# A two-layer streaming encoder in FP32 on one core: twelve of the mixer's sixteen output rows taken by seven products instead of eight

## The chip, the cores and the metric

The kernel runs on one core of one Trainium2 chip. The metric is the device time of one launch in microseconds (us). The engines are called TensorE (PE in the profile, its weight loads PEld), VectorE (DVE), ScalarE (ACT), GpSimd (POOL) and SyncE (SP, which only starts transfers here).

## The reference

Two layers work on 640 tokens (512 new frames of one stream and 16 new frames of each of eight running streams), 1024 wide. Each layer is a half-step SwiGLU block, the mixer, and a second half-step SwiGLU block; a last norm follows. The change lies in the mixer's second half:

```
z = h @ w_in                       # conv B | C | V | q | k | v | gates (2 x 1024 columns)
y_c = B * causal_depthwise_conv3(C * V)          # 512 wide
y_a = chunk-band attention(q, k, v)              # 512 wide
m = sigmoid(g_c) * (y_c @ w_conv_out) + sigmoid(g_a) * (y_a @ w_attn_out)
x += m @ w_o
```

## The kernel before

Everything is feature-major: a tile is 128 features by 640 tokens, cut into two halves of 320 tokens (`t1`, `t2`). Operands are split into a high part (a rounding copy on ACT, names ending in `hi`) and a low part (the rest, `source - hi`, on DVE, names ending in `lo`), and each product is three matmuls: high by high, high by low, low by high. One matmul is 128x128 by 128x320.

**Products by seven.** The FFN's and the mixer's input products use a 2x2 block scheme with seven block products instead of eight. A *unit* makes two output rows. It has seven blocks of 12 matmuls, 84 in all, in this order; I number them here:

| block | operand | written to (PSUM) | weights |
|---|---|---|---|
| P1 | `X11` | `pa` | w0 |
| P2 | `X21` | `pb` | w0 |
| P3 | `XN6` | `pa`, added on | w1 |
| P4 | `XT5` | `pc` | w1 |
| P5 | `XT7` | `pa`, added on | w2 |
| P6 | `X22` | `pc`, added on | w2 |
| P7 | `XT4` | `pa`, added on | w3 |

Since `pa` is added on, P3 waits until ACT has copied P1's sum out (`c1`), P5 until ACT has copied the next one (`u2`), and P7 until DVE has used P5's sum (`add(g[:, t2], pa, c5)`).

**Weights.** A unit's weights arrive as two tiles `raw` of 128x1024 (n and n + 1, three buffers in all). `source` makes sums of them on DVE, `prep` splits them into `whi` and `wlo` (three buffers each) for the slabs w0 to w3, and `slab`, `quiet` and `flush` say where in DVE's queue that is written. Of w1 the first half (the sum `s6`) serves P3, the second P4; of w2 the first half serves P5. In a mixer unit DVE makes three sums for w1 and w2's first half, and one more for w2's second half.

**The stage.** `outputs` runs with PE, DVE and ACT in the order of the program text. It makes seven gate units (`gate_pair(2)` to `gate_pair(14)`, each with two sigmoids on ACT) and 16 output rows: 8 of `y_c @ w_conv_out` (`co`), 8 of `y_a @ w_attn_out` (`ao`), each row by `out`: 24 matmuls on `py`, then a product with the gate on DVE, and for `ao` a sum into `mm`. After gate 2 come rows 0 to 3, and after each later gate unit two rows. `give` splits the eight results `mm` into the operands `m_0` to `m_7` of the last product, `po` = w_o, 48 matmuls for each of 8 rows. The tiles of `m_0` to `m_7` are those of the normalised input `h`, which the gate units' blocks P1, P2, P4 and P6 read.

Of the kernel before, what the change touches and what calls it, by code (L numbers as in the profile page):

```python
# [59 lines left out]
MARGIN = 2, 4  # L60
LEAN = {"a0": (1, 6), "b0": (1, 5), "a1": (0, 5), "b1": (1, 5)}
# [52 lines left out]
def mixer_order():  # L114

    mix = lambda *rows: ("mix", rows)
    out = [("v", None)] + [mix(("q", p), ("k", p)) for p in range(AW // P)]
    for c in range(0, CT, 2):  # L120
        out += [mix(("C", c + i), ("V", c + i)) for i in range(2)] + [mix(("B", c), ("B", c + 1))]
    gates = [mix(("g", m), ("g", m + 1)) for m in range(0, 2 * KT, 2)]
    out += gates[:2] + [("co", m) for m in range(4)]
    for i, g in enumerate(gates[2:]):
        name, m = ("co", 4 + 2 * i) if i < 2 else ("ao", 2 * i - 4)
        out += [g, (name, m), (name, m + 1)]
    return out + [("o", m) for m in range(KT)]
# [8 lines left out]
def stages():  # L136

    out, done = [], []

    def end(kind):  # L140
        done.append((kind, out[:]))
        out.clear()

    def plain(n):
        out.extend([8] * (n // 8) + [n % 8] * (n % 8 > 0))

    def ffn(name):
        held = 0
        for what, a in ffn_order(name):
            if what == "gu":  # L150
                plain(held)
                held = 0
                out.append("gu")
            elif what == "std":
                held += 2 * KT
            elif what == "cut":
                plain(held)
                held = 0
            elif what == "rows":
                plain(held)  # L160
                held = 0
                out.append("gu")
            elif what == "ends":
                held += KT * len(a)
            else:
                held += sum(len(js) for _, js in a)
        plain(held)

    for l in range(L):
        ffn(f"a{l}")  # L170
        end("ffn")
        held = 0
        for what, _ in mixer_order():
            if what == "mix":
# [12 lines left out]
def two(ps):  # L187
    return ps[:, :, :HT]
# [7 lines left out]
def trunk(ctx: ExitStack, tc: tile.TileContext, xin, wst, small, pbias, samplebias, kcache, vcache, gfin,  # L196
# [54 lines left out]
    for kind, units in stages():  # L251
# [3 lines left out]
        at += n  # L255
    raws, ready = [], []
    sums, pool, spool = {}, [None], [None]
    lent, lean, at = {}, set(), 0
    for name, (_, units) in zip([f"{k}{l}" for l in range(L) for k in "amb"], stages()):
        ns = []  # L260
        for z in units:
            if z == "gu":
                ns.append(at)
            at += 2 if z in ("gu", "mix") else 1
        if name in LEAN:
            lean.update(ns[slice(*LEAN[name])])

    def lend(n):

        z = lent[n] = pool[0].tile([P, 2, HT], F32, tag="cap", name=f"lent{n}", bufs=6).rearrange(  # L270
            "p a b -> p (a b)")[:, h1]
        POOL.dma_start(z, wst[n][:, h1])
# [20 lines left out]
    def source(i):  # L293
# [3 lines left out]
        if i not in sources:  # L297
# [4 lines left out]
            elif arg == 0:  # L302
                if n in lean and n not in lent:
                    lend(n)
                sources[i] = [(ra, whole)]
            else:
                rb = load(n + 1)
                if arg == 1 and kind == "gu":
# [5 lines left out]
                    sources[i] = [(st, whole)]  # L314
                elif arg == 1:
# [1001 lines left out]
    def mixer(l, after):  # L1317
        with tc.tile_pool(name=f"yp{l}", bufs=1, reuse_waits="tile") as yp, \
# [84 lines left out]
            with tc.tile_pool(name=f"gp{l}", bufs=1, reuse_waits="tile") as gp, \  # L1403
                 tc.manual_schedule(engines=ORDERED):
                hold[0] = True
                mo = outputs(l, gp, ops.X, st, cs, ycs, yas, sigmoid, gates)
        ex = after()
        with tc.manual_schedule(engines=ORDERED):
            hold[0] = True
            for m in range(KT):  # L1410
                po = acc(f"po{l}_{m}")
                product(po, mo)
# [56 lines left out]
    def outputs(l, gp, X, st, cs, ycs, yas, sigmoid, gates):  # L1469
# [4 lines left out]
        mm = ycs + [spare[i // 2][:, i % 2] for i in range(CT)]  # L1474
# [4 lines left out]
        def gate_pair(m, then=None):  # L1479
# [5 lines left out]
            ACT.copy(c1, pa)  # L1485
            prep(used[0] + 1)
            flush()
            block(pb, s0, 1, X21, every, True, True)
# [6 lines left out]
            ACT.copy(c5, pc)  # L1495
            s2 = slab(True)[0]
# [5 lines left out]
            if then:  # L1502
                then()
# [4 lines left out]
            sigmoid(u, m)  # L1508
# [5 lines left out]
            sigmoid(g, m + 1, -1.0)  # L1514
# [7 lines left out]
        def out(m, y, then=None):  # L1522

            py = acc(f"py{l}_{m}")
# [9 lines left out]
            flush()  # L1534

        yc, ya, mo = [], [], []

        def take(y, name, srcs):
            for c, src in enumerate(srcs):
                y.append(parts(gp, f"y{c}", f"{name}{l}_{c}", src))  # L1540
# [5 lines left out]
        gate_pair(2, lambda: take(yc, "yc", ycs))  # L1546
        for m in range(4):
            out(m, yc)
        for m in range(4, 2 * KT, 2):
            last = m == 2 * KT - 2  # L1550
            gate_pair(m, (lambda: take(ya, "ya", [yas[:, c, :] for c in range(CT)])) if m == KT else
                      (lambda: give(range(1))) if last else None)
            y = yc if m < KT else ya
            out(m, y, (lambda: give(range(1, 4))) if last else None)
            out(m + 1, y, (lambda: give(range(4, 6))) if last else None)
        give(range(6, KT))
# [520 lines left out]
def _stream(i):  # L2077
# [9 lines left out]
    for l in range(L):  # L2087
# [36 lines left out]
        for what, m in mixer_order():  # L2124
            if what == "v":
                out.append(v.reshape(KT // 2, 2, P, AW).transpose(0, 2, 1, 3).reshape(-1, P, CH))
            elif what == "mix":
# [3 lines left out]
                out.append(chunks([rows[name][a][o::2] for name, a in m for o in range(2)]))  # L2131
            else:
# [73 lines left out]
```

## Time and profile before

| what | us |
|---|---|
| median of 3 runs (2488.70 to 2489.98) | 2489.67 |
| the profiled execution's own time | 2488.93 |
| its span in the trace | 2487.1 |
| from P2's start in gate 2 to the first matmul of `po`, layer 0 (637.35 to 778.09) | 140.74 |
| the same, layer 1 (1869.15 to 2009.89) | 140.74 |

The span's own trace is used for all durations. A row of a timeline gives the start, the duration, the engine, the line, the operation and its tiles; a bracket at its end gives the idle time in front and what ended it. Successive instructions of one engine overlap a little, so what one costs its queue is the distance from its start to the next start, not its duration.

### The profile page before, as it was taken

The numbers are of one execution on the slowest core, as the hardware profiler recorded it, in microseconds if no ns is written. First come the engines' busy times: TensorE is split into PE (matmuls) and PEld (weight loads), VectorE is DVE, ScalarE is ACT, GpSimd is POOL, SyncE is SP. The second block draws the span as 40 slices with busy tenths as digits, with TensorE's granted clock in tenths as the row PEclk, the third lists the DMA queues.
The fourth block names the chain that finished last, engine by engine and source line by source line (L and its number), as shares of the span: only waits on it lengthen the run. The fifth ranks groups of instructions, "written<-read, shape, count | busy, mean of one in ns | idle before, by whom it ended". The sixth has DMA issues, their size and how long they took to land.

```text
span 2487.1 us, 43918 instructions
## 1 busy us (share of the span) xinstructions
PE 2473.8 (99%) x17312; PEld 2421.2 (97%) x17312; DVE 2140.1 (86%) x3533; ACT 1355.4 (54%) x2152; POOL 298.4 (12%) x451
## 2 busy tenths in 40 slices
PE   9999999999999999999999999999999999999999
PEld 8999999889999999999999999998999999999998
DVE  7999998888776899998799999988886769999997
ACT  6555556665444655555665555556644455555555
POOL 0111112211000001111001011121110000111111
PEclk9999999999999999999999999999999999999999
DMA  4443545335223333444334443453442232444444
GB/s 155 126 118 101 124 118 121 113 108 174 77 82 114 93 102 105 113 117 117 111 93 109 110 118 101 116 128 106 133 157 86 77 111 87 109 116 105 113 117 117
DMA packets 109934, 279.75 MB, mean 112 GB/s; under 512 B 12480, under 2 KB 52032, under 8 KB 109728
## 3 DMA queue, kind: packets, MB, share of 16 engines
q1 hardware_dynamic: 69552, 220.10, 28.0%
q0 software_dynamic: 39744, 56.60, 12.3%
q8 instruction: 135, 2.21, 0.4%
q14 instruction: 71, 0.58, 0.1%
q10 hardware_dynamic: 432, 0.25, 0.0%
HBM read 231.09 MB, written 7.94 MB: 96 GB/s over the span
## 4 chain that ended last, share of the span: by engine, by line
PE 94%; DVE 3%; ACT 2%; issue 1%; DMA 1%; SPq 0%; DVEq 0%; ACTq 0%; POOLq 0%
PE pab L442 12%; PE paa L442 11%; PE pcb L442 6%; PE daa L1127 6%; PE pca L442 5%; PE dab L1127 5%; PE po L418 5%; PE py L418 5%; PE qa L442 4%; PE pbb L442 3%; PE dca L1127 3%; PE pba L442 3%; PE dcb L1127 2%; PE ma_cv L442 2%; PE ma_qk L442 2%; PE pv L1612 2%
## 5 line engine op out<-in xcount | busy, mean ns | idle before, releaser
L352 DVE TENSOR_TENSOR wlo<-raw,whi 128x1024 fp32r<-128x1024 f32 (+1 forms) x569 | 579.9, 1021 | 155.9 <-ACT whi L347 152.8
L347 ACT CAST whi<-raw 128x1024 fp32r<-128x1024 f32 (+1 forms) x569 | 504.7, 890 | 380.1 <-PE pbb L442 47.2
L347 ACT CAST whi<-s 128x1024 fp32r<-128x1024 f32 (+1 forms) x158 | 150.3, 951 | 296.1 <-issue 111.2
L442 PE MATMUL pab<-xhib,whi 128*128 128x320 f32 x704 | 217.7, 309 | 0.0
L442 PE MATMUL pab<-xhib,wlo 128*128 128x320 f32 x704 | 217.3, 309 | 0.0
L442 PE MATMUL pab<-xlob,whi 128*128 128x320 f32 x704 | 217.3, 309 | 0.0
L442 PE MATMUL paa<-xhia,whi 128*128 128x320 f32 x640 | 197.8, 309 | 0.2 <-DVE ga L287 0.2
L442 PE MATMUL paa<-xhia,wlo 128*128 128x320 f32 x640 | 197.6, 309 | 0.0
L442 PE MATMUL paa<-xloa,whi 128*128 128x320 f32 x640 | 197.5, 309 | 0.0
L352 DVE TENSOR_TENSOR wlo<-s,whi 128x1024 fp32r<-128x1024 f32 (+1 forms) x158 | 173.5, 1098 | 4.6 <-ACT whi L347 4.6
L1149 POOL DMA_DIRECT2D x<-c_a x80 | 70.2, 1030 | 574.1 <-ACT ahia L1031 205.4
L442 PEld LDWEIGHTS pab<-xhib,whi 128*128 128x128 f32 x704 | 132.2, 188 | 0.9 <-issue 0.9
L1149 POOL DMA_DIRECT2D x<-c_b x72 | 63.2, 1013 | 582.0 <-ACT ahib L1031 205.6
L442 PEld LDWEIGHTS pab<-xlob,whi 128*128 128x128 f32 x704 | 132.2, 188 | 0.0
L442 PEld LDWEIGHTS pab<-xhib,wlo 128*128 128x128 f32 x704 | 132.2, 188 | 0.0
L442 PEld LDWEIGHTS paa<-xhia,whi 128*128 128x128 f32 x640 | 120.1, 188 | 1.1 <-DVE ga L287 0.5
L442 PEld LDWEIGHTS paa<-xloa,whi 128*128 128x128 f32 x640 | 120.2, 188 | 0.3 <-DVE xloa L686 0.3
L442 PEld LDWEIGHTS paa<-xhia,wlo 128*128 128x128 f32 x640 | 120.1, 188 | 0.2
L442 PE MATMUL pcb<-xhib,wlo 128*128 128x320 f32 x352 | 108.9, 309 | 0.0
L442 PE MATMUL pcb<-xlob,whi 128*128 128x320 f32 x352 | 108.6, 309 | 0.0
L442 PE MATMUL pcb<-xhib,whi 128*128 128x320 f32 x352 | 108.6, 309 | 0.0
L287 DVE TENSOR_TENSOR raw<-s,raw 128x512 f32<-128x512 f32 x158 | 107.9, 683 | 0.0
(764 smaller groups left out, 8077.7 us busy)
## 6 DMA issues: line engine op xcount, KB each, us to landing
raw<-in_wst SPq DMA_DIRECT2D x375, 512.0 KB, 3.6
x<-c_a POOLq DMA_DIRECT2D x80, 160.0 KB, 4.7
x<-c_b POOLq DMA_DIRECT2D x72, 160.0 KB, 3.6
lent<-in_wst POOLq DMA_DIRECT2D x36, 256.0 KB, 3.9
kc<-in_kcache SPq DMA_DIRECT2D x32, 256.0 KB, 4.9
vc<-in_vcache SPq DMA_DIRECT2D x16, 512.0 KB, 4.9
x<-u_a POOLq DMA_DIRECT2D x40, 160.0 KB, 3.9
x<-u_b POOLq DMA_DIRECT2D x36, 160.0 KB, 3.9
```

What stands on the lines that cost most here:

```text
L287: DVE.tensor_tensor(out=out, in0=a, in1=b, op=op)
L347: ACT.copy(hi[:, d], src[:, c])
L352: DVE.tensor_tensor(out=lo, in0=src, in1=hi.bitcast(F32), op=ALU.subtract)
L418: PE.matmul(ps[:, a, :HT], w, x[a] if isinstance(x, tuple) else x[:, a * HT : (a + 1) * HT], start=first and j == 0 and not seeded, stop=l ...
L442: PE.matmul(ps, a, b, start=start and kp == 0 and j == 0, stop=stop and kp == NP - 1 and j == 2, skip_group_check=True)
L1127: PE.matmul(ps[u], w, y, start=start and i == 0 and j == 0, stop=i == 1 and j == 2, skip_group_check=True)
L1149: POOL.dma_start(x[ms[2 * u + r]][:, cols], z[:, u], accum_op=ALU.add)
L1612: PE.matmul(pv[t], xx[:, t * P : (t + 1) * P], w[:, kk * AW : (kk + 1) * AW], start=c == 0 and kk == 0 and j == 0, stop=c == KT // 2 - 1 a ...
```

## The change

Rows 4 to 7 of `co` and all rows of `ao` are made by seven, four rows at a time: `rows` is a unit of 84 matmuls where four calls of `out` have 96. The order becomes gate 2, rows 0 to 3, gate 4, gate 6, `co` 4 to 7, gate 8, gate 10, `ao` 0 to 3, gate 12, gate 14, `ao` 4 to 7. The operands for it are made from `y_c` and `y_a` by `mixed` (four sums of 128x320, then splits of 128x960 and 128x320 into high and low parts), twice for each. For the nine units of weights from gate 4 on, one sum that DVE made comes from two transfers on POOL's queue, the second adding onto the first (`lend_one`), issued a unit ahead. The gates' sigmoids are put off into the next unit (`lates`, `due`), the gated rows go through a staging tile, the results of `co` 4 to 7 are copied on ACT (`moved`), and the first two rows of `po` are interleaved by halves of their sums.

```diff
+FREE = AW // P + 3 * CT // 2 + 2
...
+    out += gates[:2] + [("co", m) for m in range(4)] + gates[2:4] + [("rows", ("co", (4, 5, 6, 7)))]
+    for i in range(2):
+        out += gates[4 + 2 * i : 6 + 2 * i] + [("rows", ("ao", tuple(range(4 * i, 4 * i + 4))))]
...
+        lean.update(ns[slice(*LEAN.get(name, (FREE, None)))])
...
+    def lend_one(n):
+        z = lent[n] = apart[0].tile([P, CH // 2], F32, tag="one", name=f"one{n}", bufs=2)
         POOL.dma_start(z, wst[n][:, h1])
         POOL.dma_start(z, wst[n + 1][:, h1], accum_op=ALU.add)
...
+                elif arg == 1 and n in lean:
+                    if after_mix[n] in lean:
+                        lend_one(after_mix[n])
+                    flush()
+                    st = sums[n] = spool[0].tile([P, CH // 2], F32, tag="s6", name=f"s6_{n}", bufs=1)
+                    add(rb[:, h1], rb[:, h1], rb[:, h2])
+                    add(st, rb[:, h1], ra[:, h1])
+                    sources[i] = [(st, h1), (rb, h1)]
...
             block(pa, s0, 0, X11, every, True, True)
             ACT.copy(c1, pa)
+            due()
             prep(used[0] + 1)
             flush()
+            at[0]()
...
-            sigmoid(u, m)
+            lates.append(lambda: sigmoid(u, m))
...
+            first = [acc(f"po{l}_{m}") for m in range(2)]
+            ws = [[tiles.take() for _ in mo] for _ in first]
+            for ks in (range(KT // 2), range(KT // 2, KT)):
+                for p, w in zip(first, ws):
+                    for k in ks:
+                        multiply(p, w[k], mo[k], k == 0, k == KT - 1)
...
+        def mixed(i, y, z):
+            z = z.rearrange("p c (a b) -> p (c a) b", a=2)
+            e1, e2, o1, o2 = (z[:, i] for i in range(4))
+            add(e1, e1, e2, ALU.subtract)
+            add(e2, o2, e2, ALU.subtract)
+            for out, a in ((o2, e1), (o1, o2)):
+                DVE.scalar_tensor_tensor(out=out, in0=a, scalar=-1.0, in1=out, op0=ALU.mult, op1=ALU.subtract)
+            yield
...
+        def rows(name, ms, y, then=None):
...
+            B, A = (acc(f"r{i}{n}") for i in "ba")
+            a, b = ([z[:, u, :HT] for u in range(2)] for z in (A, B))
+            c = [att(f"rc{n}_{u}")[:, :HT] for u in range(2)]
+            s1, s2, s5 = stage
...
+            w = quiet()
+            mul(a, w, 0, X11, True)
+            ACT.copy(s1, two(A))
+            due()
+            prep(used[0] + 1)
+            flush()
+            mul(b, w, 1, X21, True)
+            add(s1, two(B), s1)
+            w = slab(True)[0]
+            flush()
+            mul(a, w, 0, XN6, False)
+            ACT.copy(s2, two(A))
+            gated(0, [s1[:, u] for u in range(2)], t1)
+            mul(c, w, 1, XT5, True)
+            for u in range(2):
+                ACT.copy(s5[:, u], c[u])
+            w = slab(True)[0]
+            mul(a, w, 0, XT7, False)
+            add(s5, two(A), s5)
+            flush()
+            ahead()
+            gated(1, [s5[:, u] for u in range(2)], t2, -1.0)
+            mul(c, w, 1, X22, False)
+            for u in range(2):
+                add(s2[:, u], c[u], s2[:, u])
+            w = slab(True)[0]
+            gated(0, [s2[:, u] for u in range(2)], t2)
+            if then:
+                then()
+            if name == "co":
+                moved(0)
+            mul(a, w, 0, XT4, False)
+            flush()
+            gated(1, a, t1, -1.0)
+            if name == "co":
+                lates.append(lambda: moved(1))
...
+        rows("co", (4, 5, 6, 7), yc)
+        z = [mixed(i, ya, yas[:, 2 * i : 2 * i + 2]) for i in range(2)]
+        pair = lambda c: (take_even(c, yas_[c]), take(ya, "ya", [c + 1], yas_))
+        go = [going(u) for u in z]
+        gate_pair(8, [lambda: pair(0), lambda: pair(2), go[0]])
+        gate_pair(10, [also(go[0], go[1]), also(go[0], go[1], go[0]), also(go[1], go[0], go[1], go[1])])
+        rows("ao", (0, 1, 2, 3), ya)
+        gate_pair(12, [lambda: total(0, 2), none, lambda: total(2, 4)])
+        gate_pair(14, [lambda: give(range(2)), none, lambda: give(range(2, 4))])
+        rows("ao", (4, 5, 6, 7), ya, lambda: total(4, 6))
+        total(6, 8)
+        give(range(4, KT))
```

The three functions given to `gate_pair` run behind P1, behind P4 and behind P5. So the queues of DVE and ACT read otherwise. The rows below are those of layer 0.

DVE before, from the sum of gate 8's P5 (`qa0_8`) on (`wlo190` is the weights of the two rows behind gate 8, `wlo191` w0 of gate 10, the last row the first of gate 10's sums; `ya0_0lo` to `ya0_3lo` are the low parts of the attention's result):

```order
L287 TENSOR_TENSOR g0_8_1_7936<-qa0_8_7932,c50_4829 128x320
L1499 TENSOR_TENSOR g0_8_1_7936<-g0_8_1_7936,rrm0_4818 128x320
L352 TENSOR_TENSOR wlo190_8001<-raw104_7998,whi190_8000 128x1024
L235 TENSOR_TENSOR ya0_0lo_8021<-ya0_4760,ya0_0hi_8020 128x640
L235 TENSOR_TENSOR ya0_1lo_8025<-ya0_4760,ya0_1hi_8024 128x640
L235 TENSOR_TENSOR ya0_2lo_8029<-ya0_4760,ya0_2hi_8028 128x640
L235 TENSOR_TENSOR ya0_3lo_8033<-ya0_4760,ya0_3hi_8032 128x640
L287 TENSOR_TENSOR g0_8_7935<-qc0_8_7934,capsm0_4817 128x320
L1507 TENSOR_TENSOR g0_8_7935<-g0_8_7935,rrm0_4818 128x640
L1513 TENSOR_TENSOR g0_8_1_7936<-qa0_8_7932,rrm0_4818 128x320
L352 TENSOR_TENSOR wlo191_8050<-raw105_8018,whi191_8049 128x1024
L287 TENSOR_TENSOR raw105_8018<-raw105_8018,raw106_8070 128x512
```

DVE now, from the second sum of the weights behind gate 8's P5 on (`wlo193` is w1 of gate 10, its first row the half that P3 waits for; `wlo194` is w2; the two pairs of `x2` rows are `mixed`):

```order
L295 TENSOR_TENSOR s6_104_8099<-raw105_8094,raw104_8074 128x512
L295 TENSOR_TENSOR ya0_4760<-ya0_4760 128x320 x2
L1597 SCALAR_TENSOR_TENSOR ya0_4760<-ya0_4760 128x320 x2
L295 TENSOR_TENSOR g0_8_7991<-qc0_8_7990,capsm0_4817 128x320
L1543 TENSOR_TENSOR g0_8_7991<-g0_8_7991,rrm0_4818 128x640
L1549 TENSOR_TENSOR g0_8_1_7992<-qa0_8_7988,rrm0_4818 128x320
L368 TENSOR_TENSOR wlo193_8120<-s6_104_8099,whi193_8119 128x512
L368 TENSOR_TENSOR wlo193_8120<-raw105_8094,whi193_8119 128x512
L295 TENSOR_TENSOR raw104_8074<-s6_104_8099,raw104_8074 128x512
L368 TENSOR_TENSOR wlo194_8161<-one104_7942,whi194_8160 128x512
L368 TENSOR_TENSOR wlo194_8161<-raw104_8074,whi194_8160 128x512
L295 TENSOR_TENSOR ya0_4760<-ya0_4760 128x320 x2
```

Before, two rows of `out` (48 matmuls) stood between gate 8 and gate 10; now gate 10 follows at once, and the sums for `mixed` stand ahead of its w1.

ACT before, around the start of gate 8 (line 1485 copies `c1`, line 1493 `u2`):

```order
L347 CAST whi187_7875<-raw103_7869 128x512
L1485 COPY capsm0_4817<-qa0_8_7932 128x320
L347 CAST whi188_7951<-raw102_7833 128x1024
L347 CAST whi189_7968<-raw103_7869 128x512
L1493 COPY capsm0_4817<-qa0_8_7932 128x320
```

ACT now at the same place, the start of gate 8 behind `co` 4 to 7 (line 1654 is `moved`, 1519 copies `c1`, 1529 `u2`):

```order
L1654 COPY yc0_0_4819<-g0_4_7588 128x640
L1654 COPY yc0_0_4819<-g0_4_1_7589 128x640
L1519 COPY capsm0_4817<-qa0_8_7988 128x320
L1654 COPY yc0_1_4820<-g0_6_7721 128x640
L1654 COPY yc0_1_4820<-g0_6_1_7722 128x640
L363 CAST whi190_8009<-one102_7810 128x512
L363 CAST whi190_8009<-raw102_7921 128x512
L234 CAST ya0_0hi_8015<-ya0_4760 128x320
L234 CAST ya0_1hi_8019<-ya0_4760 128x640
L363 CAST whi191_8036<-raw103_7940 128x512
L1529 COPY capsm0_4817<-qa0_8_7988 128x320
```

Between the two copies that gate 8's P3 and P5 wait for there stood two casts of weights; now two moves and five casts stand there.

ACT before, around the start of gate 14:

```order
L1485 COPY capsm0_4817<-qa0_14_8509 128x320
L347 CAST whi203_8528<-raw111_8408 128x1024
L347 CAST whi204_8545<-raw112_8444 128x512
L1493 COPY capsm0_4817<-qa0_14_8509 128x320
L1495 COPY c50_4829<-qc0_14_8511 128x320
```

ACT now at the same place (`m0_0hi` and `m0_1hi` are written to tiles of `h` that P4 of this very unit still reads):

```order
L1519 COPY capsm0_4817<-qa0_14_8556 128x320
L1350 ACTIVATE g0_12_8426<-g0_12_8426,sm_73 128x640
L1350 ACTIVATE g0_12_1_8427<-g0_12_1_8427,sm_73 128x640
L363 CAST whi206_8577<-one110_8379 128x512
L363 CAST whi206_8577<-raw110_8493 128x512
L234 CAST m0_0hi_8583<-mm0_0_7299 128x640
L234 CAST m0_1hi_8587<-mm0_0_7299 128x640
L363 CAST whi207_8604<-raw111_8513 128x512
L1529 COPY capsm0_4817<-qa0_14_8556 128x320
```

The first two results' casts moved ahead of the copy of `u2`, and the sigmoids of gate 12 into gate 14.

More of the change, by code (lines that the diff above doesn't have):

```diff
@@ L173, in stages @@
         for what, _ in mixer_order():
[L174 removed]
+            if what in ("mix", "rows"):
                 plain(held)
@@ new lines, in total, with also, going @@
+        def total(m0, m1):
+            for m in range(m0, m1):
+                add(mm[m], mm[m], gates[KT + m])
+        none = lambda: None
+        def also(*fs):
+            return lambda: [f() for f in fs]
+        def going(z):
+            return lambda: next(z)
+        gate_pair(2, [none, none, lambda: take(yc, "yc", range(CT), ycs)])
+        z = [mixed(i, yc, ycp[i]) for i in range(2)]
+        out(0, yc, None, going(z[0]))
+        out(1, yc, None, also(going(z[0]), going(z[1])))
```

123 lines of the change are left out of this document (91 added, 32 removed).

## The prediction

> **What bounds the kernel now.** The page first, then the busy times of the two stretches that change (P2 of gate 2 to the first matmul of `po`, layers 0 and 1), then the chain that ended last inside one of them.
>
> ```profile
> span 2487.1 us, 43918 instructions
> PE 2473.8 (99%) x17312; PEld 2421.2 (97%) x17312; DVE 2140.1 (86%) x3533; ACT 1355.4 (54%) x2152; POOL 298.4 (12%) x451
> ```
>
> ```profile
> core 0: us, PE busy (x) PEld busy (x) DVE busy (x) ACT busy (x) POOL busy (x), PEclk, DMA share, GB/s
> 637.35:778.09 140.74, 140.67 (x962) 140.44 (x960) 100.94 (x144) 65.53 (x96) 0.00 (x0) 1.00 0.27 87
> 1869.15:2009.89 140.74, 140.67 (x962) 140.44 (x960) 100.69 (x143) 65.36 (x96) 0.00 (x0) 1.00 0.26 87
> ```
>
> ```profile
> 637.35 1.76 PE qb L442 x12
> 639.11 1.76 PE qa L442 x12
> ...
> 647.90 14.08 PE py L418 x96
> ...
> 732.30 7.04 PE py L418 x48
> ```
>
> TensorE is the bound, here without a gap: 140.67 of 140.74 us, at full granted clock (1.00). DVE is busy for 100.94 us, 72%. A matmul costs 7.04 / 48 = 0.1467 us, a block of 12 1.76, a unit of 84 12.32.
>
> **What is removed.** Three groups per layer go from 96 to 84 matmuls: 36 x 0.1467 = 5.28 us, 10.56 in both layers. That is all PE can win; against it stand the waits that PE gets.
>
> **What DVE and ACT get.** Their prices are distances from start to start. DVE in a dense piece, then ACT:
>
> ```profile
> 728.89 0.49 DVE L287 TENSOR_TENSOR g<-qa,c 128x320 f32<-128x320 f32 x1 [1.01 <-PE qa L442]
> 729.42 0.49 DVE L1499 TENSOR_TENSOR g<-g,rrm 128x320 f32<-128x320 f32 x1
> 729.83 1.22 DVE L352 TENSOR_TENSOR wlo<-raw,whi 128x1024 fp32r<-128x1024 f32 x1
> 730.96 0.48 DVE L287 TENSOR_TENSOR g<-qc,capsm 128x320 f32<-128x320 f32 x1
> 731.48 0.82 DVE L1507 TENSOR_TENSOR g<-g,rrm 128x640 f32<-128x640 f32 x1
> ...
> 734.00 0.69 DVE L287 TENSOR_TENSOR raw<-raw,raw 128x512 f32<-128x512 f32 x1
> 734.72 0.69 DVE L287 TENSOR_TENSOR s<-raw,raw 128x512 f32<-128x512 f32 x1
> 735.33 0.68 DVE L287 TENSOR_TENSOR raw<-raw 128x512 f32<-128x512 f32 x1
> 735.93 0.82 DVE L1532 TENSOR_TENSOR g<-py,g 128x640 f32<-128x640 f32 x1
> 736.78 0.82 DVE L287 TENSOR_TENSOR yc<-yc,g 128x640 f32<-128x640 f32 x1
> 737.53 0.69 DVE L352 TENSOR_TENSOR wlo<-s,whi 128x512 fp32r<-128x512 f32 x1
> ```
>
> ```profile
> 708.05 1.05 ACT L347 CAST whi<-raw 128x1024 fp32r<-128x1024 f32 x1
> 708.99 0.73 ACT L234 CAST ya_0hi<-ya 128x640 fp32r<-128x640 f32 x1
> 709.62 0.73 ACT L234 CAST ya_1hi<-ya 128x640 fp32r<-128x640 f32 x1
> ...
> 719.00 0.62 ACT L347 CAST whi<-s 128x512 fp32r<-128x512 f32 x1 [1.51 <-DVE s L287]
> 719.53 0.62 ACT L347 CAST whi<-raw 128x512 fp32r<-128x512 f32 x1
> 721.79 0.43 ACT L1485 COPY capsm<-qa 128x320 f32<-128x320 f32 x1 [1.64 <-PE qa L442]
> ```
>
> On DVE 320 columns cost 0.41 us (729.42 to 729.83), or 0.53 where the next instruction needs the result (728.89 to 729.42); 512 cost 0.61 or 0.72, 640 0.74 (736.78 to 737.53) or 0.85, 1024 1.13. On ACT 512 cost 0.53, 640 0.63, 1024 0.94, 320 (not shown alone) about 0.33 as duration less the same 0.1. `mixed` and the gated rows bring two forms that this stretch lacks, which the trace has elsewhere:
>
> ```profile
> 1254.55 1.16 DVE L686 TENSOR_TENSOR xloa<-xoa,xhia 128x960 fp32r<-128x960 f32 x1 [0.32 <-ACT xhia L617]
> 1255.63 0.69 DVE L352 TENSOR_TENSOR wlo<-lent,whi 128x512 fp32r<-128x512 f32 x1
> 1256.23 0.69 DVE L352 TENSOR_TENSOR wlo<-raw,whi 128x512 fp32r<-128x512 f32 x1
> L1154 DVE SCALAR_TENSOR_TENSOR x<-dab,x 128x320 f32<-128x320 f32 x12 | 5.3, 484 | 0.7 <-PE dab L1127 0.5
> ```
>
> 960 columns cost 1.08; the scalar form of 320 columns lasts 0.484, as the plain one. By the order DVE does 52 more instructions of 320 columns, 30 more of 512, 4 of 960, and 8 fewer each of 640 and 1024 per layer: 52 x 0.45 + 30 x 0.61 + 4 x 1.08 - 8 x 0.76 - 8 x 1.13 = +31 us. So DVE has some 101 + 31 = 132 us of work in 140.74 - 5.28 = 135.5. The lent sums are already taken off in this (one of 512 less in each of six gate units, 6 x 0.61 = 3.7 us). The share alone stalls nothing; where the work stands does.
>
> How a late result of DVE or ACT reaches PE is seen once in the FFN:
>
> ```profile
> 1256.33 0.31 PE L442 MATMUL pca<-xloa,whi 128*128 128x320 f32 x1
> 1256.97 0.42 PE L442 MATMUL pca<-xhia,wlo 128*128 128x320 f32 x1 [0.33 <-DVE wlo L352]
> 1257.22 0.31 PE L442 MATMUL pca<-xhia,whi 128*128 128x320 f32 x1
> ```
>
> The low half ended at 1256.92, the held matmul started 0.05 later, and the one behind it came 0.25 after that instead of 0.15. So a matmul whose input ends at time t starts at t + 0.05, and 0.11 more is lost. The low half is first used by a block's third matmul, so it may end 0.13 after the block's due start; an ACT copy must end 0.16 ahead of it. From a block's end to DVE's first use of its sum go 0.27 us, counted from the next block's start:
>
> ```profile
> 728.62 0.31 PE L442 MATMUL qc<-hhim,whi 128*128 128x320 f32 x1
> ```
>
> (728.62 to 728.89, where DVE stood waiting.)
>
> **Five places, per layer.** *1. DVE from gate 8's P5 to P3 of `ao` 0 to 3.* PE passes 24 + 84 + 24 = 132 matmuls, 19.36 us; less 0.27, plus 0.13, DVE has 19.2. In that it must do 36 instructions: 19 of 320 columns (10 held by their forerunner: 5.3 + 3.7), 11 of 512 (two held, the last in full: 7.0), two each of 640, 960 and 1024 (1.5 + 2.2 + 2.3), and it waits 0.1 for a cast: 22.1. PE waits 2.9, part before gate 10's P3, part before that of `ao`. What hid such work before was the 48 matmuls of `py` between two gates, now gone.
>
> *2. ACT into gate 8.* From P5 of `co` 4 to 7, DVE reaches the last gated product that `moved` needs after 0.74 + 1.13 + 0.72 + 0.61 + 6 x 0.41 + 2 x 0.61 + 0.49 = 7.4; behind it ACT does two moves, two casts of 512, one of 320, one of 640, one of 512 and the copy of `u2`: 3 x 0.63 + 3 x 0.53 + 0.33 + 0.43 = 4.24. Gate 8's P5 is due 72 matmuls after the first P5, 10.56 - 0.27 - 0.16 = 10.1. Wait: 11.6 - 10.1 = 1.5.
>
> *3. P3 of gate 14 and of `ao` 4 to 7.* From P5's sum to the low half of the next w1 DVE does 7.26 us (the gate's own 5.78 and two of 640: totals, or the low parts of `m_2`, `m_3`); PE needs it after 48 matmuls, 7.04 - 0.27 + 0.13 = 6.9. Twice 0.36 = 0.7. A unit without extras has 5.78 and a group of rows 6.4: no wait.
>
> *4. P5 of gate 14.* `m_0`'s tile is free after 15 matmuls from P3's start (2.2 + 0.2 us); then two casts of 640, one of 512 and the copy: 2.2 us, end at 4.6; P5 is due at 3.52 - 0.16. Wait 1.3.
>
> *5. The second row of `po`.* It takes the PSUM of `ao` 4 to 7 and waits for the last gated product. Behind P5 DVE does 0.74 + 1.13 + 2 x 0.41 + 4 x 0.41 + 2 x 0.8 + 1.13 + 0.41 + 0.49 = 8.0; due after 48 matmuls, 7.04 - 0.27 - 0.16 = 6.6. Wait 1.3. The interleaving itself then hides `m_4` to `m_7`: their low parts come 0.74 apart, PE needs one per 6 matmuls, 0.88.
>
> Sum 2.9 + 1.5 + 0.7 + 1.3 + 1.3 = 7.7, both layers 15.4, against 10.56: +4.8 us. The profiled execution was 2488.93 us (2487.1 span and 1.8 around it) and becomes 2493.8; the median is 0.74 above it: **2494.5 us**, slower by 0.2%, which is also what a measurement of this kernel can tell from no change.
>
> What I cost at nothing. POOL's lent sums: their like in the FFN has this row.
>
> ```profile
> lent<-in_wst POOLq DMA_DIRECT2D x36, 256.0 KB, 3.9
> ```
>
> Two in turn take 7.8 us and the issue, within the unit of 12.32 by which they are ahead; POOL had 0.00 us to do in the stretch and nothing else is queued there. If they came later than that, w2's cast would stand in ACT's queue, and P5 with it, by the excess. Everything before gate 8: by the same prices DVE has 14.5 us of work beside the 14.08 of the four `py` rows, with gate 2's slack ahead of them, and in gates 4 and 6 one sum less than before. The put-off sigmoids: their results are used a unit later at the earliest. SP's queue has the same loads as before.
>
> **The skill.** The Trainium skill, "VectorE: DVE Perf Modes", section "The DRAIN you can't avoid", says that the next DVE operation does not start until the pipe is empty, semaphore or not. The rows agree only where the next needs the result (0.53 for 0.49); elsewhere the start comes 0.08 earlier, and its own note on instructions that are not held leaves room for that. By the rule place 1 would take the full durations, 23.5 us instead of 22.1.
>
> **The rivals.** *Faster.* Only the two waits behind ACT's queue (places 2 and 4) stay, because DVE runs further ahead than my start at P5 allows: 2 x 2.8 = 5.6 against 10.56, 2484.7 or below. It decides if DVE's 36 instructions take 19 us instead of 22, 0.53 each for 0.61. For it: three buffers of split weights. Against: the distances repeat to 0.01, and P5's sum holds the queue in each unit. 0.10. *Half of it.* Some waits overlap, 8 to 13 us in all: 2487 to 2492. 0.20. *Full durations.* Place 1 takes 9.3 + 7.5 + 1.6 + 2.3 + 2.4 + 0.4 = 23.5 and the others 0.5 more each: 3.3 per layer, 2501. Against: the rows above. 0.03. *Late tiles.* With three `raw` buffers the second tile of a unit is loaded only when DVE has done the w2 before it, 2.7 us into the unit; its sum starts at 7.4.
>
> ```profile
> raw<-in_wst SPq DMA_DIRECT2D x23, 512.0 KB, 3.4
> vc<-in_vcache SPq DMA_DIRECT2D x16, 512.0 KB, 4.9
> ```
>
> At 3.4 us to landing 1.3 are left; beside the lent transfers (256 KB twice) it may be 4.9 or more, then 0.3 in each of six units, 3.6 in all: 2498. 0.12. *The forecast*, 2492 to 2497: 0.55.
>
> **The numbers.** Slower by over 0.2% (above 2494.65) takes half of the forecast's case and some, and both slow rivals: 0.46. Within 0.2%: the other half and the half case, 0.43. Faster 0.11. The range runs from 2487.5 to 2499.
>
> **What would show it.** In the changed trace the stretch should last 135.5 + 7.7 = 143 us, DVE over 90% busy from gate 8 to gate 12, with PE waiting for `wlo` (DVE) at P3 of gate 10 and of `ao`, for ACT's `u2` copy at P5 of gates 8 and 14, and for DVE at `po`'s second row. If PE shows no gap there, the time is 2479; if it waits for a transfer, the late tiles are right.

## The result, and the profile after

The changed kernel takes 2492.38 us (median of 20 runs, 2491.87 to 2493.58) against 2489.11 for the kernel before (20 runs): a ratio of 1.0014, 95% interval 1.0008 to 1.0020. It is slower by 3.3 us, less than the 0.2% set as the bound; the forecast was 2494.5, the range 2487.5 to 2499.0.

The page of the profiled execution, then the two stretches from P2 of gate 2 to the first matmul of `po` and the part of layer 0 from gate 8 to gate 12 (columns as in the view of before: length, then busy time of PE, PEld, DVE, ACT and POOL):

```profile
span 2491.8 us, 44037 instructions
PE 2468.9 (99%) x17240; PEld 2411.7 (97%) x17240; DVE 2193.9 (88%) x3671; ACT 1392.0 (56%) x2236; POOL 323.6 (13%) x487
```

```profile
638.40:779.61 141.21, 137.71 (x926) 135.34 (x925) 125.26 (x207) 81.95 (x135) 10.05 (x14) 1.00 0.38 109
1872.11:2013.63 141.52, 138.03 (x926) 135.62 (x925) 126.41 (x209) 82.46 (x135) 10.06 (x14) 1.00 0.38 109
699.80:740.81 41.01, 38.56 (x255) 36.98 (x253) 38.78 (x69) 25.70 (x44) 4.30 (x6) 1.00 0.44 118
```

The 72 matmuls are gone (17312 to 17240), and yet the stretch lasts longer than the 140.74 us of before. DVE went from 100.94 to 125.26 us, and between gate 8 and gate 12 it is busy for 38.78 of 41.01 us, 95%.

Where TensorE lost time is read best from its weight loads. Matmuls follow each other every 0.147 us but last 0.31, so part of a delay disappears in their overlap; a load lasts 0.19. The last matmul ahead of one wait, and the two behind it:

```profile
730.40 0.31 PE L1640 MATMUL rbao<-ya_3hi,wlo 128*128 128x320 f32 x1
731.14 0.41 PE L1640 MATMUL raao<-xhi,whi 128*128 128x320 f32 x1 [0.43 <-ACT capsm L1658]
731.39 0.30 PE L1640 MATMUL raao<-xlo,whi 128*128 128x320 f32 x1
```

The held matmul starts 0.59 us late, and the next one comes 0.25 behind it instead of 0.147: 0.70 us are lost. The matmul's own bracket says 0.43, that of its load 0.70. These are all the brackets of the timeline of PEld in layer 0 from gate 8 to the second row of `po`:

```profile
703.60 0.19 PEld L458 LDWEIGHTS qa<-thi,whi 128*128 128x128 f32 x1 [0.39 <-ACT capsm L1519]
708.15 0.19 PEld L458 LDWEIGHTS qa<-thi,whi 128*128 128x128 f32 x1 [1.02 <-ACT capsm L1529]
718.04 0.19 PEld L458 LDWEIGHTS qa<-thi,wlo 128*128 128x128 f32 x1 [0.80 <-DVE wlo L368]
721.63 0.19 PEld L458 LDWEIGHTS qa<-thi,whi 128*128 128x128 f32 x1 [0.37 <-ACT capsm L1529]
731.14 0.19 PEld L1640 LDWEIGHTS raao<-xhi,whi 128*128 128x128 f32 x1 [0.70 <-ACT capsm L1658]
732.20 0.19 PEld L1640 LDWEIGHTS raao<-xhi,wlo 128*128 128x128 f32 x1 [0.76 <-DVE wlo L368]
757.13 0.19 PEld L458 LDWEIGHTS qa<-thi,wlo 128*128 128x128 f32 x1 [0.30 <-DVE wlo L368]
761.59 0.19 PEld L458 LDWEIGHTS qa<-thi,whi 128*128 128x128 f32 x1 [1.23 <-ACT capsm L1529]
770.99 0.19 PEld L1640 LDWEIGHTS raao<-xhi,wlo 128*128 128x128 f32 x1 [0.30 <-DVE wlo L368]
784.24 0.30 PEld L434 LDWEIGHTS po<-m_0hi,whi 128*128 128x128 f32 x2 [1.22 <-issue]
```

L1519 and L1529 are ACT's copies `c1` and `u2` of a gate, L1658 the first copy of a group of rows, L368 the low part of weights on DVE; the last, "issue", waits for the last gated product (the matmul's own row names DVE `g`). They add up to 7.1 us, and the view of waits gives the same 7.1 for layer 1. The first nine, 5.87 us, lie in the stretch and account for its length: 140.74 less the 5.28 removed, less 0.3 lost before (shown below), plus 5.87 is 141.0; measured are 141.2 and 141.5. All ten belong to the five chains of the forecast, but three stand at waits that it did not name: P3 of gate 8, P5 of gate 10, and ACT's copy ahead of P3 of `ao`. They lie on the way to the end of a chain, for which the forecast gives the whole delay, so they are added up here:

| place | forecast | measured |
|---|---|---|
| 1: P3 and P5 of gate 10, P3 of `ao` 0 to 3 | 2.9 | 0.80 + 0.37 + 0.70 + 0.76 = 2.6 |
| 2: P3 and P5 of gate 8 | 1.5 | 0.39 + 1.02 = 1.4 |
| 3: P3 of gate 14 and of `ao` 4 to 7 | 0.7 | 0.30 + 0.30 = 0.6 |
| 4: P5 of gate 14 | 1.3 | 1.2 |
| 5: second row of `po` | 1.3 | 1.2 |

What the forecast left out is a wait that the kernel before has and the changed one hasn't. In the same view of the kernel before, PE's loads wait 0.5 us per layer at `po`, 0.3 of it ahead of its first matmul:

```profile
PEld po L418 <- issue: 0.3, 1, 0.3
PEld po L418 <- DVE m_6lo L235: 0.2, 1, 0.2
```

The 0.3 shows in the forecast's own row, where PEld is busy for 140.44 of 140.74 us; it read "without a gap" from the matmuls.

So the account is 2 x (7.1 - 0.5) - 10.6 = +2.6 us; the medians give +3.3, and what makes the 0.7 between them stays open. The two profiled spans differ by 4.7, as the profiled execution of the changed kernel is 1.2 us above its median. It reached P2 of gate 2 at 638.40 instead of 637.35, 1.05 us late in code that the change leaves alone, and lost 0.4 more just ahead of layer 1's P2 of gate 2, where DVE waits for a tile of weights:

```profile
1868.72 0.69 DVE L295 TENSOR_TENSOR raw<-raw,raw 128x512 f32<-128x512 f32 x1 [1.36 <-DMA raw<-in_wst]
1870.35 0.19 PEld L458 LDWEIGHTS qa<-hhim,whi 128*128 128x128 f32 x1 [0.42 <-ACT ya L1999]
```

### The profile page after: what moved, and what is told of

Same layout as the page of the kernel before. It is cut to its first block, busy times and chain, and to the rows that moved or that the text cites. A ratio compares the mean times of both kernels' runs of the same rounds, so it can differ in the third digit from the quotient of the medians.

```text
span 2491.8 us, 44037 instructions
## 1 busy us (share of the span) xinstructions
PE 2468.9 (99%) x17240; PEld 2411.7 (97%) x17240; DVE 2193.9 (88%) x3671; ACT 1392.0 (56%) x2236; POOL 323.6 (13%) x487
## 3 DMA queue, kind: packets, MB, share of 16 engines
q0 software_dynamic: 43776, 66.04, 14.2%
## 4 chain that ended last, share of the span: by engine, by line
PE 87%; DVE 7%; issue 3%; ACT 2%; DMA 1%; DVEq 0%; ACTq 0%; POOLq 0%
PE pab L458 12%; PE paa L458 10%; PE pcb L458 6%; PE daa L1143 5%; PE dab L1143 5%; PE pca L458 5%; PE po L434 4%; PE pbb L458 3%; PE qa L458 3%; PE dca L1143 3%; PE pba L458 2%; PE dcb L1143 2%; PE ma_qk L458 2%; PE pv L1781 2%; PE ma_cv L458 2%
## 5 line engine op out<-in xcount | busy, mean ns | idle before, releaser
L363 ACT CAST whi<-raw 128x512 fp32r<-128x512 f32 (+1 forms) x581 | 503.4, 871 | 378.1 <-PE pbb L458 46.0
L368 DVE TENSOR_TENSOR wlo<-raw,whi 128x512 fp32r<-128x512 f32 (+1 forms) x581 | 577.9, 997 | 135.8 <-ACT whi L363 131.4
L368 DVE TENSOR_TENSOR wlo<-s,whi 128x1024 fp32r<-128x1024 f32 (+1 forms) x164 | 177.5, 1082 | 4.4 <-ACT whi L363 4.4
```

The costliest lines, as they stand in the source:

```text
L363: ACT.copy(hi[:, d], src[:, c])
L368: DVE.tensor_tensor(out=lo, in0=src, in1=hi.bitcast(F32), op=ALU.subtract)
```

## The experiments

Each run changes the changed kernel, unless said otherwise, and is compared with runs of the kernel before on the same chip (their medians lie between 2488.88 and 2489.01). The changed kernel's 2492.38 was measured beside 2489.11, so a difference to it is good to some 0.2 us.

**Place 2 alone.** The products of the convolution's rows go where the copies would have moved them:

```diff
+                    o = mm[ms[2 * r + u]][:, t] if name == "co" else g
-                        DVE.tensor_tensor(out=g, in0=src[u], in1=g, op=ALU.mult)
+                        DVE.tensor_tensor(out=o, in0=src[u], in1=g, op=ALU.mult)
...
-            if name == "co":
-                moved(0)
```

The later copies, `moved(1)`, go in the same way.

> The last step of the convolution's gated rows writes its product straight to where the mixer sums it up, so ACT's four copies of 640 columns per layer (each 0.63 us, two of them ahead of the first copy of gate 8, two ahead of its second) are gone; DVE and TensorE do the same work. My theory (place 2 is ACT's queue, and it is one place of several that add up): the wait at P3 of gate 8 (0.40 us with its restart) goes, and that at P5 (1.02) falls to about 0.5, since the cast ahead of the second copy waits for a sum that stands in DVE's queue: 0.9 us per layer, 1.8 in all, about 2490.6. Rival one, the moves alone make place 2: 1.42 per layer, 2489.5. Rival two, DVE is the bound from gate 8 to the gated rows, so what TensorE gains here it waits for at gate 10 and at the rows: no change, 2492.4.

Measured: 2490.44 us, 1.9 less than the changed kernel; ratio to before 1.0007 (0.9998 to 1.0016). PEld's timeline has no bracket at P3 of gate 8 any more, and at P5:

```profile
706.14 0.19 PEld L458 LDWEIGHTS qa<-thi,whi 128*128 128x128 f32 x1 [0.65 <-ACT capsm L1529]
```

My theory: 1.41 became 0.65. The rest is the cast ahead of the copy, which waits for a sum in DVE's queue.

**Place 5 alone.** `rows("ao", (4, 5, 6, 7), ya)` without `total(4, 6)` inside, and `total(4, 8)` behind it.

> Behind the last gate, DVE adds up the totals of rows 4 and 5 (2 x 0.74 us) behind the last gated product instead of ahead of it; everything else stays. My theory (place 5): the second row of po waits for that product alone, so its wait, 1.23 us with the restart, goes: 2.5 us in both layers, about 2489.9. Rival: the low parts of m_4 to m_7 come no earlier than now and the first row asks for them 1.2 us earlier, so half of it comes back there: 1.2 us, 2491.2. If the wait is not DVE's queue but the product itself: no change.

Measured: 2489.59 us, 2.8 less; ratio 1.0002 (0.9993 to 1.0011). The wait at `po` is gone from the view, the others stand as they were. The low parts of `m_4` to `m_7` did not take it back.

**Place 4 alone.**

```diff
-        gate_pair(14, [lambda: give(range(2)), none, lambda: give(range(2, 4))])
+        gate_pair(14, [none, lambda: give(range(2)), lambda: give(range(2, 4))])
```

> In gate 14 the casts of m_0 and m_1 stand behind ACT's third copy instead of ahead of the second; DVE's two low parts move with them. My theory (place 4): P5 no longer waits for the second copy, 1.25 us per layer; but DVE now does the two low parts between P4's end and P5's sum and is about 0.8 late for that sum, which shows at P3 of the gated rows behind it, where the wait grows from 0.30 to about 1.1: net 0.5 per layer, 1.0 in all, about 2491.4. Rival: DVE's idle 1.07 us ahead of P5's sum takes both low parts, and all 2.5 us are won, 2489.9.

Measured: 2490.70 us, 1.7 less; ratio 1.0008 (0.9999 to 1.0017). P5 of gate 14 has no bracket; P3 of the rows behind it has two, 1.03 for 0.30:

```profile
768.48 0.19 PEld L1640 LDWEIGHTS raao<-xhi,whi 128*128 128x128 f32 x1 [0.27 <-ACT capsm L1658]
769.53 0.19 PEld L1640 LDWEIGHTS raao<-xhi,wlo 128*128 128x128 f32 x1 [0.76 <-DVE wlo L368]
```

So most of the wait moved from one place to the next, as the theory gave (1.1): 0.5 us per layer are won by the trace, 0.8 by the medians.

**Place 1, by POOL.** In `mixed`, for the attention's half, `POOL.tensor_tensor` (four) and one `POOL.tensor_scalar` in place of DVE's four operations.

> The eight sums of 320 columns per layer that make the inputs of the attention's gated rows are done by POOL instead of DVE (five operations for each half, since the subtraction with a factor of -1 is split), so DVE has 4.0 us less to do between P5 of gate 8 and P3 of the gated rows. My theory (place 1 is DVE's work against 19.2 us): all of its 2.65 us per layer go, 5.3 in all, about 2487.1. Rival one: POOL is several times slower than DVE, 2 us or more for 320 columns; then the second half's sums end behind the time at which ACT casts them, ACT's queue stands, and the copy for P5 of gate 10 with it: no gain, or slower than 2492.4. Rival two: place 1 is made by the order, not by the work, and the gain is the part at P3 of gate 10 alone, 0.80 per layer, 2490.8.

Measured: 2496.99 us, 4.6 more; ratio 1.0031 (1.0019 to 1.0043). The outcome is rival one's, but not by its price of 2 us, and neither side had that DVE would become slower. The waits from P7 of gate 8 to P3 of the rows come to 4.1 us in layer 0, for 2.6. Rows of the timelines of POOL and DVE, the last from the changed kernel, where POOL does nothing beside it:

```profile
711.04 1.33 POOL L1598 TENSOR_TENSOR ya<-ya 128x320 f32<-128x320 f32 x1
714.20 1.15 POOL L1595 TENSOR_TENSOR ya<-ya 128x320 f32<-128x320 f32 x1
```

```profile
710.14 1.50 DVE L235 TENSOR_TENSOR ya_3lo<-ya,ya_3hi 128x640 fp32r<-128x640 f32 x1
711.57 0.48 DVE L295 TENSOR_TENSOR g<-qa,c 128x320 f32<-128x320 f32 x1
714.02 1.89 DVE L295 TENSOR_TENSOR raw<-raw 128x512 f32<-128x512 f32 x1
```

```profile
712.33 0.69 DVE L295 TENSOR_TENSOR raw<-raw 128x512 f32<-128x512 f32 x1
```

POOL needs 1.0 to 1.4 us for what DVE does in 0.48, and while it works, DVE's operations with both inputs in SBUF are 0.1 to 1.2 us longer (1.89 for 0.69 at most); `g<-qa,c`, with one input in PSUM, keeps its 0.48. The Trainium skill, "SBUF — State Buffer", section "Who interferes with whom", has this rule: a DVE instruction with two SBUF inputs contends with a GpSimd instruction that reads SBUF, one with at most one SBUF input doesn't, outside the 2-port perf modes, which `tensor_tensor` lacks. The trace agrees in both halves (1.89 for 0.69, and 0.48 as before).

**Place 1, on DVE.** Four sums of 640 columns for both halves, in gate 10; only `XN6`'s low part ahead of P3 of the rows:

```diff
-                low(lo, z[:, 1:], hi)
+                low(lo[:, 2], z[:, 3], hi[:, 2])
...
-        gate_pair(10, [also(go[0], go[1]), also(go[0], go[1], go[0]), also(go[1], go[0], go[1], go[1])])
+        gate_pair(10, [lambda: sums7([zz[:, :, k] for k in range(4)]), also(go[0], go[0], go[1], go[0]),
+                       also(go[1], go[0], go[1], go[1])])
```

> Place 1 by other means: the same sums and low parts stay on DVE, but the sums of both halves are four operations of 640 columns instead of eight of 320 (about 3.2 us for 4.0), and of the two low parts of 960 columns only the 320 that P3 of the attention's gated rows reads stay ahead of it; the other four of 320 are done behind it, two ahead of P5 and two ahead of P7 of those rows. DVE's chain from P5 of gate 8 to P3 of the rows is 22.1 - 0.75 - 1.34 = 20.0 us against 19.2. My theory (work against time): of 2.65 us some 0.8 are left, 1.85 us per layer, 3.7 in all, about 2488.7. Rival: the low parts that are put off come back as a wait at P5 or P7 of the rows or at P3 of gates 12 and 14; then at most the 0.75 of the sums is won, 1.5 in all, 2490.9.

Measured: 2492.55 us, no gain; ratio 1.0015 (1.0006 to 1.0024). Neither side had the sizes right: place 1 only fell from 2.6 to 2.3 us, and 0.7 came back at P7 of the rows, P5 of gate 12 and P3 of gate 14, partly where the rival had it. DVE did the sums in 3.3 us as worked out, but its timeline now holds two waits for ACT inside the chain, 1.48 us:

```profile
717.12 0.69 DVE L368 TENSOR_TENSOR wlo<-one,whi 128x512 fp32r<-128x512 f32 x1 [0.70 <-ACT whi L363]
724.99 1.23 DVE L368 TENSOR_TENSOR wlo<-raw,whi 128x1024 fp32r<-128x1024 f32 x1 [0.78 <-ACT whi L363]
```

The first cast stands behind the put-off sigmoids, the second behind the casts of the sums, which I had moved ahead of it. A chain that runs through DVE and ACT isn't shortened by DVE's share alone.

**All five places.** The edits of places 1, 2 and 5, with `total(2, 4)` in gate 14, `give(range(2))` behind its third copy, `give(range(2, 4))` in the rows behind it, and one cast of 640 put behind gate 8's second copy.

> All five places at once: gated products of the convolution written straight to their place (no moves), one cast of 640 put behind the second copy of gate 8, the lighter chain of DVE as in the run before, the totals of rows 2 and 3 put off into gate 14, the casts of m_0 and m_1 behind the third copy of gate 14 and those of m_2 and m_3 into the gated rows behind it, the totals of rows 4 to 7 behind the last gated product. My theory (five separate waits, 7.15 us per layer as measured, of which 0.8 stay at place 1 and 0.3 to 0.5 at place 5): 6 us per layer are won, about 2480.5, between 2479 and 2483; TensorE's own work alone is 2489 - 10.6 = 2478.5. Rival: DVE is saturated over the whole stretch and only hands its lateness on from place to place; then the gain is no more than what single edits gave, 3 to 6 us in all, 2486 or above.

Measured: 2485.62 us, 6.8 less than the changed kernel and 0.14% faster than before, ratio 0.9986 (0.9977 to 0.9995). It lies outside the range of the theory and 0.4 below the rival's bound. The waits of layer 0 fell from 7.1 to 3.7 us, not to 1.3. Places 2 to 5 are nearly gone; place 1 is about as it was in the run before (2.6 us for 2.3), with the same 0.78 us of DVE waiting for a cast, and DVE gets to P5's sum of gate 8 late, by low parts that stand there now.

**Place 1 again.** The casts of the sums go behind the weights' cast, and the low parts of the attention's outputs come earlier, two in the convolution's rows, inside which the tiles that they overwrite come free, and two early in gate 8:

```diff
-        rows("co", (4, 5, 6, 7), yc)
+        rows("co", (4, 5, 6, 7), yc, mid=lambda: [take_even(c, yas_[c]) for c in (0, 2)], end=odd)
...
-        gate_pair(8, [lambda: take_even(0, yas_[0]), lambda: (take(ya, "ya", [1], yas_), pair(2)), none])
+        gate_pair(8, [odd_low, none, none])
```

> The run with all places changed, with two causes taken away that its trace shows at place 1: DVE's own waits for ACT (0.78 us for the cast of 1024 columns that stood behind the casts of the sums; now those come behind it), and its start 1.1 us late at P5 of gate 8 (the low parts of the attention's outputs; now the casts of all four are done in the convolution's gated rows, where the old tiles come free after P4 and P6, two low parts of 320 in DVE's idle time there and two of 640 early in gate 8). My theory (place 1 is DVE's work of 20.0 us against 19.2 plus these two): of the 3.7 us of waits per layer that the run with all places has left, 0.8 at place 1 and 0.5 at place 5 stay, 2.3 us per layer are won, 4.6 in all, about 2481.0, between 2480 and 2483. Rival: DVE is at its limit over the stretch and the wait only moves, to P3 of gate 8 or of the rows: less than 1.5 us in all, above 2484.

Measured: 2482.54 us, ratio 0.9975 (0.9964 to 0.9985): faster than the kernel before by 0.25%, and 9.8 us less than the changed kernel. All waits of layer 0 in PEld's view:

```profile
PEld raao L1652 <- DVE wlo L368: 0.8, 1, 0.8
PEld raao L1652 <- ACT capsm L1671: 0.5, 1, 0.5
PEld po L434 <- issue: 0.4, 1, 0.4
PEld qa L458 <- ACT capsm L1529: 0.3, 1, 0.3
PEld qa L458 <- DVE wlo L368: 0.2, 1, 0.2
```

2.2 us are left, 1.3 of them at place 1, where DVE still waits 0.67 us for the cast behind the sigmoids. The theory had 1.3 left in all; it held to 1.5 us of the time.

**The lent sums.** First the changed kernel without them (`lean` without the mixers).

> The changed kernel without the transfers that lend one weight sum per unit in the mixers: DVE does that sum of 512 columns (0.61 us) again in each of six gate and row units per layer, POOL's transfers there are gone. My theory: the two units in place 1's chain add 1.2 us, gates 12 and 14 and the rows behind them 0.6 each at P3 as far as they have no slack, together 2.5 us per layer, 5 in all, about 2497.5. Rival: each unit has slack for one more sum, or the transfers cost DVE as much elsewhere: no change, 2492.4.

Measured: 2508.22 us, 15.8 more; ratio 1.0077 (1.0064 to 1.0090), three times what I expected. The expectation counted six units per layer. The changed kernel's page has 36 such transfers, two for each unit and so nine units per layer:

```profile
one<-in_wst POOLq DMA_DIRECT2D x36, 256.0 KB, 4.0
```

That is 9 x 0.61 = 5.5 us of DVE's work per layer, 11 in all. DVE's waits for casts of weights, this kernel first and then the changed one, layer 0:

```profile
DVE wlo L369 <- ACT whi L364: 11.4, 11, 1.4
```

```profile
DVE wlo L368 <- ACT whi L363: 3.6, 6, 1.0
```

So the next run does the sums on DVE, but casts in two halves, `[(ra, h1), (ra, h2)]` for `[(ra, whole)]`.

> The run without the lent sums cost 15.8 us where 5 were expected. Its trace shows DVE idle for 11.4 us in the stretch of layer 0 waiting for casts of weights, against 3.6 in the changed kernel: the half that was lent had been cast while DVE still worked on the other half's sum, and without it one cast of 1024 columns waits for that sum and DVE waits for the cast. Here the lent sums stay off and DVE does the sums, but the cast is split in two of 512 again, so that the first half, whose sum DVE has done a unit earlier, is cast ahead of the second half's sum. My theory (the cast's place, not the sum, made two thirds of it): about 2497.5, the 5 us of the six sums of 0.61 us per layer as first worked out. Rival: the sums themselves cost it, because each one comes where the chain has no slack: 2505 to 2508.

Measured: 2501.09 us, ratio 1.0049 (1.0035 to 1.0063); DVE's wait for casts is 1.5 us. The time lies between the two sides. The cast's place was 7.1 us of the 15.8. The other 8.7 go with the sums, eighteen rather than the twelve for which I had 5: the sum in the convolution's rows also makes the moves late, and with them the copy that P3 of gate 8 waits for (1.1 us for 0.4), and P3 of gate 14 and of the rows behind it waits 1.1 and 1.0 us, for 0.3 each.

Then the kernel before with the lent sums alone.

> The kernel before with the lent sums alone: in six units per layer of the two mixers one sum of 512 columns (0.61 us of DVE) is replaced by two transfers of 256 KB a unit ahead, and all rows stay plain. My theory: the stretch has no gap on TensorE, so work taken off DVE there is worth nothing, and POOL, which had nothing to do there, hides the transfers: 2489.0, within 0.5. Rival: the transfers disturb the weight loads on the other queue or take DVE's port, and TensorE gets waits: 2490 or more.

Measured: 2489.19 us, ratio 1.0001 (0.9992 to 1.0010). Where TensorE waits for next to nothing (0.5 us per layer), taking work off DVE is worth nothing, and the transfers cost nothing that shows.

**The convolution's rows alone.** The attention's rows plain, two behind each gate. Other than the text says, `po` kept the two interleaved rows.

> One part alone: the convolution's last four rows by seven as in the changed kernel (12 matmuls fewer per layer), the lent sums kept, but all eight of the attention's gated rows plain, two behind each gate, with po as before the change. It removes 2 x 1.76 = 3.5 us of TensorE's work. My theory: of the five places only the wait for ACT at gate 8 can stay, 0.4 us at P3 and up to 0.1 at P5, since the casts of the attention's outputs no longer stand ahead of the second copy: 0.4 to 0.5 per layer, so about 2489.0 - 3.5 + 0.9 = 2486.4. Rival: the places are not tied to the attention's rows; then three more microseconds per layer stay and it is slower than the kernel before, 2492.

Measured: 2487.57 us, ratio 0.9995 (0.9986 to 1.0004). The view of layer 0:

```profile
PEld po L434 <- DVE g L1569: 0.6, 1, 0.6
PEld qa L458 <- ACT capsm L1519: 0.4, 1, 0.4
PEld po L434 <- issue: 0.3, 1, 0.3
```

P3 of gate 8 keeps its 0.4 and P5 has none, as expected; the 0.6 at `po` comes from the interleaving that I had left in. So the 12 matmuls of the convolution (1.8 us per layer) are had for a wait of 0.4, while the 24 of the attention's rows (3.5 us) brought the rest of the 7.1.

**One account for all runs.** TensorE's floor is 2489.0 less the removed matmuls and less before's 1.0 us of waits; to it come the waits of both layers in PEld's view:

| run | waits, layers 0 + 1 | floor + waits | measured |
|---|---|---|---|
| changed kernel | 7.1 + 7.1 | 2491.6 | 2492.38 |
| no moves (2) | 6.3 + 6.3 | 2490.0 | 2490.44 |
| totals last (5) | 5.9 + 5.9 | 2489.2 | 2489.59 |
| casts later (4) | 6.6 + 6.6 | 2490.6 | 2490.70 |
| sums on POOL (1) | 8.6 + 8.8 | 2494.8 | 2496.99 |
| less on DVE (1) | 7.3 + 7.3 | 2492.0 | 2492.55 |
| all places | 3.7 + 3.7 | 2484.8 | 2485.62 |
| chain on time | 2.2 + 2.2 | 2481.8 | 2482.54 |
| convolution alone | 1.3 + 1.3 | 2487.1 | 2487.57 |
| no lent sums | 14.3 + 14.3 | 2506.0 | 2508.22 |
| no lent sums, split cast | 11.2 + 11.2 | 2499.8 | 2501.09 |

The waits are those of one profiled execution, the times are medians. Waits ahead of P2 of gate 2 are left out of layer 1: 0.4 us for the changed kernel, 0.2 for the runs without lent sums, and 1.8 for the convolution alone, whose profiled execution took 2489.97 us, with DVE waiting 2.7 us there for a tile of weights. Up to some 7 us of waits per layer the account is 0.1 to 0.8 us low; with more it falls short by 1.3 to 2.2.

## Why the prediction was right

**The bound and the saving.** Right: 72 matmuls of 0.1467 us, 10.6 us, at full clock; up to some 7 us of waits per layer, each run's time is that floor and its waits to 0.8 us.

**The five places.** Right in chain and size: 7.7 forecast, 7.1 measured, each term 0.1 to 0.3 too large. Undoing 2, 4 and 5 one at a time moved the time as the trace said, to 0.7 us, and undoing all of them brought it below the kernel before, so these waits are the cause. Place 3 was not undone alone, and place 1 fell by half only together with the others. At place 1, DVE's 36 instructions take 21.9 us, from 710.27 to 732.14, for 22.1 forecast:

```profile
710.27 0.48 DVE L295 TENSOR_TENSOR g<-qa,c 128x320 f32<-128x320 f32 x1
731.46 0.68 DVE L368 TENSOR_TENSOR wlo<-s,whi 128x512 fp32r<-128x512 f32 x1
```

The price was right but not the road: of its 2.6 us, 1.1 reach PE through ACT. The first copy of the rows waits for DVE's read of the buffer it writes, which stands late in the same chain:

```profile
730.39 0.69 ACT L1658 COPY capsm<-raao 128x640 f32<-128x640 f32 x1 [1.13 <-DVE g L295]
```

**What was off.** The forecast is 2.1 us high. Three errors make 2.8: 1.2 the five terms (2 x 0.6), 1.0 the wait at `po` in the kernel before, 0.5 per layer, which the sum did not credit, and 0.6 the base, since the median of 3 runs was 2489.67 and that of 20 is 2489.11. The 0.7 that the account leaves open goes the other way; that much of the closeness is luck. The likeliest verdict, slower by over 0.2% (0.46), did not come; within 0.2% (0.43) did. The sign of 143 us for the stretch counted place 5, which stands behind the stretch's end; without its 1.3 it is 141.9, against 141.2 and 141.5.

What removes the wait at `po` is shown in part: the run with the convolution's rows alone has the interleaving and keeps the 0.3 ahead of the first matmul, so the interleaving can account for the other 0.2 at most.

**Costs put at nothing.** Right for POOL's transfers (the run with them alone), for everything ahead of gate 8 and for the sigmoids' results. For the lent sums the prediction took 3.7 us off DVE's work per layer, those of the six gate units; with the three units of rows they are worth 5.5, and without them the kernel is slower by 15.8 us, since they also let half a cast run ahead.

**The rivals.** *Faster* fell: all five places wait, not two. *Half of it* gave 2487 to 2492 by 8 to 13 us of waits; the time came out just above, but the waits were 14.2. *Full durations* would make place 1 23.5 - 19.2 = 4.3; it is 2.6, so the distances in the rows decide. The rival is the rule of the Trainium skill, "VectorE: DVE Perf Modes", section "The DRAIN you can't avoid", without the section's own note that a next instruction which isn't held starts earlier; the trace agrees with the note (21.9 us for the 36, not 23.5). *Late tiles* fell: in no layer does PE or DVE wait for a transfer in the stretch. The late tile just ahead of it in layer 1 comes and goes between the runs (DVE waits 0 to 2.7 us for it); the kernel before shows none there, and whether the change makes it late is not shown.

## What to carry to other kernels

Where an engine runs without a gap, price a saving on it together with the deadlines of the engines that feed it: for each block, how long from the last input that they need to the result it waits for, against the time it now leaves them. A total share (DVE 72% to 89% here) does not show this; the order in each queue does, and a cast or copy that is queued behind something late is late as well. The idle brackets of the weight loads add up to the loss, so one trace shows what each wait costs. What undoing it wins is another matter: of the 1.2 us at place 4, 0.7 came back at the next place.

## What was not expected of the hardware

Beside POOL's sums, DVE's operations with two inputs in SBUF took 0.1 to 1.2 us longer, as shown. In the same run TensorE's granted clock (sixth figure after the length) fell to 0.57 in gate 10, with matmuls 0.267 us apart instead of 0.147:

```profile
720.00:724.00 4.00, 4.00 (x17) 4.00 (x18) 3.60 (x6) 3.08 (x6) 1.40 (x2) 0.57 0.11 19
```

Ahead of it the weight loads have brackets of 0.81, 1.44 and 0.83 us within 8 us, none longer. The run without lent sums and with the split cast has the same fall in both layers, behind brackets of 1.44 and 0.76 us:

```profile
735.50:739.50 4.00, 4.00 (x19) 4.00 (x18) 3.93 (x7) 2.67 (x5) 0.00 (x0) 0.57 0.22 72
1974.50:1978.50 4.00, 4.00 (x18) 4.00 (x18) 3.94 (x8) 2.69 (x6) 0.00 (x0) 0.57 0.16 43
```

A mean clock of 0.57 over 4 us is 1.7 us of full speed lost each time. That execution took 2505.14 us, 4.1 above its run's median. The waits alone do not decide it: in layer 1 of POOL's run the brackets are 0.80, 1.45 and 0.82 us, and the clock stays at 1.00. The Trainium skill, "TensorE: Matmul & The Clock Gate", section "What's actually happening", has the clock fall after an idle window of about 3.4 us; here no single wait comes near that. What decides it isn't settled by these runs. It is a cost that the account above does not hold: with 1.7 us for each fall it gives 2496.5 for the profiled execution of POOL's run, which took 2497.24, and 2503.2 for the 2505.14.
